# Latent attention with the values of two pairs of heads issued together, TensorE's order written by hand, and finished blocks parked in DRAM

## The chip, the cores and the metric

The kernel runs on one core of a Trainium2 chip. The metric is the device time of one execution in microseconds, lower is better; the median of several executions is compared between kernels.

## The reference

Two trunk layers of a diffusion backbone over 1024 latent tokens and 256 context tokens, width 1024, all in float32. Layer 0 mixes tokens by windowed grouped-query attention, layer 1 by gated linear attention, and each is followed by a squared-ReLU MLP. The change concerns layer 0's attention of the latent tokens alone:

```
def attend_block(args):                       # one block of 128 queries; 8 latent blocks
    q, k, v, blk = args                       # 16 query heads, 4 key/value heads of 64
    s_lat = einsum('bqhgd,bkhd->bhgqk', q, k)      # 3 * 128 keys: the block and its neighbours
    s_lat = where(in_window & in_sequence, s_lat, NEG_INF)
    s_ctx = einsum('bqhgd,bkhd->bhgqk', q, k_ctx)  # and all 256 context keys
    p = softmax_with_sink(concatenate([s_lat, s_ctx], -1), sink)
    return einsum(p_lat, v) + einsum(p_ctx, v_ctx)
y_lat = o_lat @ w_o
```

## The kernel before

Tokens are cut into ten blocks of 128: blocks 0 and 1 are context, 2 to 9 latent. First come the projections to queries, keys and values of all blocks, with the context blocks' own attention woven in (the listing's `ctx_rounds`), then the latent attention (`attention`), then the output projection with its residual and norm, block by block (`mixing`), then the MLP and layer 1.

`attention` is a generator that runs over 64 "pairs". A pair is one block `i`, one half `p` of the key/value heads and one `i4`; it holds two query heads (`e` = 0, 1) that use two key/value heads. One block has eight pairs. At step `t` it emits

- `scores` of pair t: for each of the two heads four matmuls (two parts of the query against the latent and the context keys) into a tile `sc` of two PSUM banks, of which there are two in all; VectorE then masks and takes the row's extreme (line 750), ScalarE takes the exponential (line 755), and GpSimd and ScalarE make the denominator;
- `divided` of pair t-1: VectorE's reciprocal (line 765), GpSimd's scaling of the probabilities (line 767);
- `turned` of pair t-3 (`LAG_T` = 3): ten transposes on TensorE (line 783; eight where the block has four key tiles), four, four and two of them into three banks `pt`, which VectorE (the first, line 786) and ScalarE (the others, line 788) empty into `pT`;
- `values` of pair t-4: ten (or eight) float32 matmuls on half of the array's columns each (the form 128*64 in the trace), two records each, into bank `o`, which gathers four pairs and is emptied by ScalarE into `oT[i]` (line 812);
- side work: once for four pairs the transposes of the next queries (bank `qt`, line 671, emptied by ScalarE at line 676 and twice by VectorE at line 680), once for eight those of further keys (`kt`), and on some steps a piece of the modulation sums (`mod_sums`, VectorE line 310) which at t = 30 and t = 62 ends in sixteen transposes `modT` (line 331).

The banks `pt`, `o`, `qt`, `kt` and `modT` come out of one pool of four (`ps1`). Working tiles of 4 KB for each partition come out of one pool of 45 (`u`); `oT[i]` holds one of them from the block's first half until its projection.

Who sets the order: the program is laid out by a planner that simulates it and gives each engine its ready instruction of highest rank, so instructions of one engine may stand in another order than they are emitted. Inside `manual_schedule(engines={PE})` TensorE's instructions keep the order in which they are emitted among themselves; instructions emitted outside may still be put between them, and the other engines stay with the planner. In the kernel before, the last three blocks' projections, with the first two steps of `attention`, lie in such a region; the remaining steps (`for _ in latents: pass`) do not.

Of the kernel before, what the change touches and what calls it, by code (L numbers as in the profile page):

```python
# [11 lines left out]
F32 = mybir.dt.float32  # L12
# [6 lines left out]
P = 128  # L19
# [6 lines left out]
NT = NC_T + NL_T  # L26
# [13 lines left out]
LAG_T = 3  # L40
# [124 lines left out]
class Backbone:  # L165
# [627 lines left out]
    def values(self, i, p, i4, pT):  # L793
        nc = self.nc
        ktiles = self.block(i)[4]
        if i4 == 0:
            self.po[i, p] = self.ps1("o")
        po = self.po[i, p]
        for n, tile_i in enumerate(ktiles):
            for e in range(2):  # L800
                g = 2 * p + e
                nc.tensor.matmul(  # L802
                    po[64 * e : 64 * (e + 1), P * i4 : P * (i4 + 1)],
                    self.kv[tile_i // 2][:, tile_i % 2, 256 + HD * g : 256 + HD * (g + 1)],
                    pT[e, n],
                    start=(n == 0),
                    stop=(n == len(ktiles) - 1),
                )
        if i4 == 3:
            if p == 0:  # L810
                self.oT[i] = self.u((P, 8, P), s="oT")
            nc.scalar.copy(self.oT[i][:, 4 * p : 4 * (p + 1), :], po.rearrange("p (a b) -> p a b", a=4))


    def scores_ctx(self, i, p, c, qs):
# [69 lines left out]

    def attention(self, steps, weights, o_ready):

        pairs = [(i, p, i4) for i in range(NC_T, NT) for p in range(2) for i4 in range(4)]
        qs, probs, pT = self.qs, {}, {}
        side = []  # L890
        for t in range(len(pairs) + LAG_T + 1):
            if t < len(pairs):
                i, p, i4 = pairs[t]
                probs[t] = self.scores(i, p, i4, qs[i, p])
            if 1 <= t <= len(pairs):
                self.divided(probs[t - 1])
            if 0 <= t - LAG_T < len(pairs):
                pT[t - LAG_T] = self.turned(pairs[t - LAG_T][0], probs.pop(t - LAG_T)["probs"])
            if 0 <= t - LAG_T - 1:
                self.values(*pairs[t - LAG_T - 1], pT.pop(t - LAG_T - 1))  # L900
            if t < len(pairs) and i4 == 0:

                nxt = (i, 1) if p == 0 else (i + 1, 0)
                q = self.queries(qs, *nxt) if nxt[0] < NT else []
                k = self.keys(i + 2) if p == 1 and i + 2 < NT else []
                side = [k[0:1], q[0:1] + k[1:2], q[1:2] + k[2:3], q[2:3] + k[3:4]]
                if p == 0 and i + 1 < NT:
                    self.q_back(i + 1)
            for f in side.pop(0) if side else ():
                f()  # L910
            if t in steps:
                steps[t]()
            if t >= len(pairs) - 20 and t % 4 == 0 or t >= len(pairs):
                weights.load()
            if t == len(pairs) - 1:
                o_ready()
            yield
# [539 lines left out]
    def gla_running(self, head, g, logs):  # L1457
# [5 lines left out]
        for d, lg in enumerate(logs):  # L1463
            run = self.half("run")[:, :w]
            r3 = run.rearrange("p (c t) -> p c t", t=P)
            l3 = lg.rearrange("p (c t) -> p c t", t=P)
            tot, mid = self.tot[head][:, d, self.chunks(g)], self.mid[head][:, d, self.chunks(g)]
            if d == 0:
                nc.vector.tensor_tensor_scan(run, self.reset[:, :w], lg, 0.0, ALU.mult, ALU.add)
                nc.vector.tensor_copy(mid, r3[:, :, 63])  # L1470
                nc.vector.tensor_copy(tot, r3[:, :, P - 1])
            else:
                nc.vector.memset(run[:, 0:1], 0.0)
                nc.vector.tensor_tensor_scan(
                    run[:, 1:w], lg[:, 0 : w - 1], self.reset[:, 1:w], 0.0, ALU.add, ALU.mult
                )
                nc.vector.tensor_copy(mid, r3[:, :, 64])
                nc.vector.tensor_tensor(tot, r3[:, :, P - 1], l3[:, :, P - 1], op=ALU.add)
            nc.vector.tensor_tensor(r3, r3, mid.unsqueeze(2).to_broadcast([P, nch, P]), op=ALU.subtract)
            if g > 0 or d == 0:  # L1480
                ex = self.u((P, 2, 512), s="ex")
            up, down = (ex[:, 0, :], ex[:, 1, :]) if g else (None, ex[:, d, :w])
            sgn = 1.0 if d == 0 else -1.0
            nc.scalar.activation(down, run, AF.Exp, scale=-sgn / TAU)
            if g > 0:
                nc.scalar.activation(up, run, AF.Exp, scale=sgn / TAU)
            res.append((up, down))
# [189 lines left out]
    def run(self):  # L1677
        nc, t = self.nc, self.t
        self.gm, self.pre = {}, {}
        self.q, self.oT = {}, {}  # L1680
        groups = [[0, 1], [2, 3, 4, 5], [6, 7, 8, 9]]


# [25 lines left out]
        def o_ready():  # L1709
            ready["rows"] = [self.gate_rows(0, 0, s) for s in range(2)]  # L1710
            ready["o"] = parts(0)
            ready["x"] = self.x_in(0)

        def parts(i):
            hi, lo = self.u((P, KT, P), F32R, "oh"), self.u((P, KT, P), F32R, "ol")
            self.split(self.oT[i], hi, lo)
            return hi, lo

        self.qs, self.qd = {}, {}
        latents = self.attention(steps, wo, o_ready)  # L1720
# [12 lines left out]
        with self.tc.manual_schedule(engines={mybir.EngineType.PE}):  # L1733
# [31 lines left out]
                    self.rotary(i)  # L1765
                    self.q_out(i)
            assert not ctx
        for _ in latents:
            pass
        rows = ready["rows"]  # L1770
        later = self.const([P, 768], "later", tag="rope")
        self.gnorm, self.junk = later[:, :DV], later[:, DV:].bitcast(mybir.dt.bfloat16)
# [1 line left out]
        h1 = MlpIn(self, 0, groups[1:], Acts(self, [[0, 1]]))  # L1774

        def mixing(tiles, parts, wo, x_of, row_of, keep, h, l, o, x, last):

            tiles = list(tiles)
# [18 lines left out]
            for s in range(n):  # L1797
                if s + 1 < n:
                    o[s + 1] = parts(tiles[s + 1])
                    x[s + 1] = x_of(tiles[s + 1])  # L1800

                def between():
                    if s >= 1:
                        residual(s - 1)
                    if s >= 2:
                        onward(s - 2)
                    if s >= 1:
                        normed(s - 1)

                y[s] = self.out_proj(o.pop(s), wo, between)  # L1810
                last(n - 1 - s)
# [4 lines left out]
        pairs = [(i, i + 4) for i in groups[1]]  # L1816
# [278 lines left out]
```

## Time and profile before

| what | us |
|---|---|
| median of three executions | 2607.4 (2607.23 to 2610.37) |
| the profiled execution, its own time | 2610.2 |
| its span | 2608.5 |
| the latent attention within the span | about 245 to 522 |

The span is the time from the first to the last instruction of the program. A stretch "284:317" is given in microseconds from the start of the span. PE stands for TensorE's matmuls, PEld for its weight loads, DVE for VectorE, ACT for ScalarE, POOL for GpSimd, SP for the queue that issues most transfers. Matmuls overlap in the records, so their spacing, from start to start, tells more than their durations.

### The profile page before, as it was taken

To read this page: it belongs to the slowest core of one execution; us is meant where nothing else is said; L and a number is where in the kernel's file an instruction comes from. 1 tells how busy PE (TensorE), PEld (TensorE's weight loads), DVE (VectorE), ACT (ScalarE), POOL (GpSimd) and SP (SyncE) were. 2 spreads that over 40 slices of the span, in tenths; PEclk is the share of its full clock that TensorE was granted. 3 is DMA by queue.
4 is the path that set the end of the run, shared out by engine and by line. 5 is a ranking of instruction groups with operands and counts; after the bars stand their busy time and mean duration, and the time that the engine had idled before them with its cause. 6 is when DMAs were issued, how large, how long until landed. Compare 5 with 4: busy or idle time off the path is not lost.

```text
span 2608.5 us, 36262 instructions
## 1 busy us (share of the span) xinstructions
PE 2543.1 (97%) x13523; PEld 2116.2 (81%) x13523; DVE 1714.7 (66%) x2607; ACT 1258.2 (48%) x2356; POOL 430.8 (17%) x720
## 2 busy tenths in 40 slices
PE   7999999999999999999999999999998999999998
PEld 5778888888888888788878888888887888878886
DVE  4775888757767665758868625636658656566676
ACT  3345777744644444433325535334446545445333
POOL 0354666411000000000002212212310000000002
PEclk9999999999999999999999999999999999999999
DMA  9210011222455565837245331102321554567474
GB/s 312 89 65 33 26 56 54 82 81 85 145 158 158 183 209 167 292 113 266 89 147 193 129 91 51 32 18 97 97 97 49 180 160 134 177 246 235 161 226 161
DMA packets 229856, 348.62 MB, mean 134 GB/s; under 512 B 24600, under 2 KB 123184, under 8 KB 229680
## 3 DMA queue, kind: packets, MB, share of 16 engines
q1 hardware_dynamic: 227088, 336.87, 39.8%
q0 software_dynamic: 2592, 9.44, 0.9%
q8 instruction: 106, 1.74, 0.3%
q14 instruction: 70, 0.57, 0.1%
HBM read 270.75 MB, written 75.50 MB: 133 GB/s over the span
## 4 chain that ended last, share of the span: by engine, by line
PE 85%; DVE 5%; DMA 4%; ACT 2%; issue 2%; POOL 1%; SPq 1%; DVEq 0%; POOLq 0%; ACTq 0%
PE p L229 7%; PE p L228 7%; PE p L230 6%; PE pa L229 4%; PE pa L228 4%; PE pa L230 4%; PE o L802 3%; PE y L230 3%; PE y L228 3%; PE y L229 3%; PE rp L228 2%; PE rp L229 2%; PE rp L230 2%; PE pc L228 2%; PE pc L230 2%; PE pt L783 2%
## 5 line engine op out<-in xcount | busy, mean ns | idle before, releaser
L229 PE MATMUL p<-ol,oh 128*128 128x512 f32 x896 | 350.7, 391 | 0.1
L230 PE MATMUL p<-oh,ol 128*128 128x512 f32 x896 | 347.2, 391 | 0.0
L228 PE MATMUL p<-oh 128*128 128x512 f32 x896 | 329.6, 392 | 4.9 <-ACT oh L212 4.1
L241 POOL TENSOR_SCALAR rs<-ss 128x1 f32<-128x1 f32 (+1 forms) x78 | 26.5, 340 | 1641.9 <-ACT later L235 1458.9
L213 DVE TENSOR_TENSOR ol<-wh,oh 128x1024 fp32r<-128x1024 f32 x128 | 153.5, 1222 | 94.3 <-ACT oh L212 93.9
L228 PEld LDWEIGHTS p<-oh 128*128 128x128 f32 x896 | 168.6, 189 | 44.1 <-ACT oh L212 5.4
L229 PEld LDWEIGHTS p<-ol,oh 128*128 128x128 f32 x896 | 168.9, 189 | 36.5 <-DVE ol L213 1.0
L230 PEld LDWEIGHTS p<-oh,ol 128*128 128x128 f32 x896 | 168.9, 189 | 35.3 <-issue 0.2
L212 ACT CAST oh<-wh 128x1024 fp32r<-128x1024 f32 x128 | 131.4, 1050 | 132.0 <-DVE wh L1212 27.6
L310 DVE SCALAR_TENSOR_TENSOR ma<-wm,cT,ma 128x1024 f32<-128x1024 f32 x112 | 147.2, 1345 | 47.0 <-DMA wm<-in_w_mod 47.0
L212 ACT CAST oh<-k 128x1024 fp32r<-128x1024 f32 x96 | 98.0, 1053 | 127.3 <-DMA k<-in_w_mlp_out 60.2
L213 DVE TENSOR_TENSOR wi<-wi,wi 128x512 fp32r<-128x512 f32 x176 | 116.6, 688 | 47.3 <-ACT wi L212 45.5
L1042 ACT COPY s<-pa 128x512 f32<-128x512 f32 x96 | 56.0, 585 | 185.5 <-PE pa L230 185.4
L767 POOL TENSOR_SCALAR pr<-pr,den 128x640 f32<-128x640 f32 (+2 forms) x160 | 124.3, 790 | 29.4 <-DVE den L765 16.6
L213 DVE TENSOR_TENSOR ol<-k,oh 128x1024 fp32r<-128x1024 f32 x96 | 113.9, 1224 | 21.2 <-ACT oh L212 17.3
L212 ACT CAST wi<-wi 128x512 fp32r<-128x512 f32 x176 | 103.4, 615 | 34.7 <-DMA hd<-h 20.9
L755 ACT ACTIVATE pr<-pr,nm 128x640 f32<-128x640 f32 (+1 forms) x128 | 102.5, 802 | 28.2 <-DVE nm L750 26.3
L228 PE MATMUL y<-woh,oh 128*128 128x512 f32 x288 | 113.9, 396 | 0.0
L230 PE MATMUL y<-woh,ol 128*128 128x512 f32 x288 | 112.4, 391 | 0.9 <-DVE ol L213 0.9
L229 PE MATMUL y<-wol,oh 128*128 128x512 f32 x288 | 112.2, 390 | 0.0
L229 PE MATMUL rp<-wgl,ah 128*128 128x512 f32 x288 | 112.1, 390 | 0.0
L230 PE MATMUL rp<-wgh,al 128*128 128x512 f32 x288 | 111.9, 390 | 0.0
(391 smaller groups left out, 6745.3 us busy)
## 6 DMA issues: line engine op xcount, KB each, us to landing
wm<-in_w_mod SPq DMA_DIRECT2D x96, 512.0 KB, 4.4
hd<-h SPq DMA_DIRECT2D x80, 512.0 KB, 3.0
wh<-hd SPq DMA_DIRECT2D x144, 256.0 KB, 3.7
wh<-in_w_mlp_out SPq DMA_DIRECT2D x144, 256.0 KB, 4.2
wi<-in_w_mlp_in SPq DMA_DIRECT2D x64, 512.0 KB, 5.0
k<-hd SPq DMA_DIRECT2D x80, 256.0 KB, 5.4
k<-in_w_mlp_out SPq DMA_DIRECT2D x80, 256.0 KB, 5.4
x<-in_x SPq DMA_DIRECT2D x16, 512.0 KB, 4.3
```

The lines of the kernel that those rows point to most:

```text
L212: self.nc.scalar.copy(hi, src)
L213: self.nc.vector.tensor_tensor(lo, src, hi.bitcast(F32), op=ALU.subtract)
L228: mm(out, a[0], b[0], start=start, stop=False, skip_group_check=onto)
L229: mm(out, a[0], b[1], start=False, stop=False, skip_group_check=onto)
L230: mm(out, a[1], b[0], start=False, stop=stop, skip_group_check=onto)
L241: nc.gpsimd.tensor_scalar(r, ss, inv_n, EPS, ALU.mult, ALU.add)
L310: nc.vector.scalar_tensor_tensor(acc[s], raw, c, acc[s], ALU.mult, ALU.add)
L755: nc.scalar.activation(pr, pr, AF.Exp, bias=nm[:, e : e + 1], scale=-1.0, accum_out=sums[:, e : e + 1])
L767: nc.gpsimd.tensor_scalar(pr, pr, den[:, e : e + 1], 0.0, ALU.mult, ALU.add)
L783: nc.tensor.transpose(pt[:, P * j : P * (j + 1)], probs[e][:, P * kt : P * (kt + 1)], self.ident)
L802: nc.tensor.matmul(po[64 * e : 64 * (e + 1), P * i4 : P * (i4 + 1)], self.kv[tile_i // 2][:, tile_i % 2, 256 + HD * g : 256 + HD * (g + 1) ...
L1042: nc.scalar.copy(s["s", j], s["pa"])
```

## The change

Three edits. `values` of pairs t-5 and t-4 are emitted together on every second step, in place of one on every step; the steps of the latent attention that were left to the planner are put into a region in which TensorE keeps the order of emission; and blocks 1 to 7 are written to DRAM (`od[i]`) when they are finished and read back into a fresh tile when `parts(i)` splits them for their projection. Blocks 0, 8 and 9 stay in SBUF. No arithmetic is added or removed.

```
@@ values
             nc.scalar.copy(self.oT[i][:, 4 * p : 4 * (p + 1), :], po.rearrange("p (a b) -> p a b", a=4))
+            if p == 1 and 0 < i < NT - 2:
+                self.od[i] = self.dp.tile([P, 8, P], F32, name=f"od{i}")
+                nc.sync.dma_start(self.od[i], self.oT.pop(i))
@@ attention
-            if 0 <= t - LAG_T - 1:
-                self.values(*pairs[t - LAG_T - 1], pT.pop(t - LAG_T - 1))
+            if t >= LAG_T + 2 and (t - LAG_T) % 2 == 0:
+
+                for n in (t - LAG_T - 2, t - LAG_T - 1):
+                    self.values(*pairs[n], pT.pop(n))
@@ run
-        self.q, self.oT = {}, {}
+        self.q, self.oT, self.od = {}, {}, {}
@@ run, parts
-            self.split(self.oT[i], hi, lo)
+            if i in self.od:
+                self.oT[i] = self.u((P, 8, P), s="oT")
+                nc.sync.dma_start(self.oT[i], self.od[i])
+            self.split(self.oT.pop(i), hi, lo)
@@ run
-        for _ in latents:
-            pass
+        with self.tc.manual_schedule(engines={mybir.EngineType.PE}):
+            for _ in latents:
+                pass
```

## Rows read from the trace of the kernel before

**Rows 1.** The page: busy time, share of the span and instructions of each engine, whole program.

```profile
PE 2543.1 (97%) x13523; PEld 2116.2 (81%) x13523; DVE 1714.7 (66%) x2607; ACT 1258.2 (48%) x2356; POOL 430.8 (17%) x720
```

**Rows 2.** Busy time of each engine by stretch. Each stretch is one latent block (eight pairs), from one emptying of bank `o` to another. Columns as the first line says.

```profile
core 0: us, PE busy (x) PEld busy (x) DVE busy (x) ACT busy (x) POOL busy (x), PEclk, DMA share, GB/s
284.00:317.00 33.00, 33.00 (x319) 28.96 (x319) 25.09 (x52) 24.83 (x67) 18.06 (x37) 1.00 0.12 36
317.00:352.00 35.00, 33.80 (x319) 28.89 (x318) 29.89 (x65) 27.04 (x72) 28.00 (x48) 1.00 0.16 50
352.00:390.00 38.00, 37.32 (x336) 31.22 (x335) 31.19 (x64) 25.04 (x65) 19.15 (x36) 1.00 0.15 43
390.00:423.00 33.00, 33.00 (x317) 28.63 (x316) 26.27 (x56) 25.45 (x68) 19.14 (x37) 1.00 0.17 49
423.00:455.00 32.00, 31.38 (x315) 27.73 (x314) 27.70 (x56) 26.36 (x68) 21.84 (x37) 1.00 0.25 67
455.00:488.00 33.00, 31.21 (x317) 27.24 (x317) 28.25 (x64) 26.95 (x68) 21.05 (x36) 1.00 0.17 47
```

**Rows 3.** TensorE's weight loads in order of time, around three turns from transposes to values and back. Columns: start, length of the run of equal instructions, engine, line, operation, tiles, shape, count, and in brackets the idle time before and what ended it.

```profile
352.69 1.12 PEld L783 LDWEIGHTS pt<-ident,pr 128*128 128x128 f32 x10
353.97 1.07 PEld L802 LDWEIGHTS o<-pT,kv 128*64 128x64 f32 x20 [0.16 <-issue]
355.21 0.30 PEld L736 LDWEIGHTS sc<-kl,qs 128*128 128x128 f32 x2 [0.17 <-issue]
...
356.39 0.90 PEld L783 LDWEIGHTS pt<-ident,pr 128*128 128x128 f32 x8
357.46 0.19 PEld L802 LDWEIGHTS o<-pT,kv 128*64 128x64 f32 x2 [0.17 <-issue]
```

**Rows 4.** The view of waits, stretch 245:522: who waited for whom, us in total, times, longest.

```profile
DVE den L765 <- POOL den L759: 16.3, 12, 1.9
...
PEld o L802 <- issue: 12.2, 72, 0.4
...
PEld pt L783 <- POOL pr L767: 5.2, 10, 1.2
...
PEld sc L736 <- DVE nm L750: 2.3, 9, 0.6
...
PEld sc L736 <- ACT pT L788: 1.7, 1, 1.7
```

**Rows 5.** Groups of instructions in the stretch 245:560: busy us, mean ns of one, and idle time of the engine before them.

```profile
L671 PE MATMUL qt<-ident,q 128*128 128x128 f32 x60 | 9.3, 278 | 0.0
...
L213 DVE TENSOR_TENSOR ol<-oT,oh 128x1024 fp32r<-128x1024 f32 x6 | 7.3, 1236 | 3.3 <-ACT oh L212 3.3
L212 ACT CAST oh<-oT 128x1024 fp32r<-128x1024 f32 x6 | 6.2, 1043 | 0.0
L331 PE MATMUL modT<-ident,ma 128*128 128x128 f32 x32 | 5.0, 279 | 0.0
```

**Rows 6.** TensorE's matmuls in order of time: the first visit to the values within the stretch (it is the context's), a turn of the next queries with what follows it, and the last visit. Columns as in rows 3.

```profile
244.78 1.09 PE L802 MATMUL o<-pT,kv 128*64 128x128 f32 x16
...
343.62 0.60 PE L671 MATMUL qt<-ident,q 128*128 128x128 f32 x4
344.06 0.60 PE L783 MATMUL pt<-ident,pr 128*128 128x128 f32 x4
...
344.95 0.66 PE L783 MATMUL pt<-ident,pr 128*128 128x128 f32 x4
345.54 1.31 PE L802 MATMUL o<-pT,kv 128*64 128x128 f32 x18
...
348.05 0.38 PE L783 MATMUL pt<-ident,pr 128*128 128x128 f32 x2
...
520.63 1.09 PE L802 MATMUL o<-pT,kv 128*64 128x128 f32 x16
```

**Rows 7.** ScalarE and VectorE at the same place, and after the transposes of rows 3: who empties the banks `qt` and `pt`, and when.

```profile
344.25 1.17 ACT L676 CAST qs<-qt 64x512 fp32r<-64x512 f32 x2 [1.24 <-PE qt L671]
...
345.75 0.69 DVE L786 COPY pT<-pt 128x512 f32<-128x512 f32 x1
...
346.46 1.39 DVE L680 TENSOR_TENSOR qs<-qt,qs 64x512 fp32r<-64x512 f32 x2
...
354.07 0.69 DVE L786 COPY pT<-pt 128x512 f32<-128x512 f32 x1
354.16 0.83 ACT L788 COPY pT<-pt 128x512 f32<-128x512 f32 x2
```

**Rows 8.** TensorE at the end of the sixteen transposes of a modulation vector.

```profile
370.56 0.60 PE L331 MATMUL modT<-ident,ma 128*128 128x128 f32 x4
371.84 1.25 PE L783 MATMUL pt<-ident,pr 128*128 128x128 f32 x8 [0.68 <-DVE S L332]
```

**Rows 9.** SP's queue, stretch 245:560: what its longest group of waits waited for (us in total, times, longest).

```profile
SPq L297 <- PE pt L783: 78.0, 7, 19.1
```

**Rows 10.** Transfers issued in 245:640: KB each, median us from issue to landing.

```profile
q<-qd SPq DMA_DIRECT2D x4, 512.0 KB, 3.3
```

**Rows 11.** The chain that ended last, at the start of two following blocks' norms in the output projection: start us, us, what.

```profile
539.86 0.87 PE xt L438 x8
...
551.64 0.87 PE xt L438 x8
```

## The prediction

> **What bounds the kernel now.** I read the page's engine line first: TensorE is busy for 97% of the span, the next engine for 66% [rows 1]. Then the table by stretch, to see whether that holds where the change is. In the six latent blocks from 284 to 488 us the granted clock is full, TensorE has hardly an idle microsecond, VectorE is busy for 168.4 of the 204 us and ScalarE for 155.7 [rows 2]. So TensorE sets the pace there too; one block of eight pairs takes 34 us, four pairs 17.0.
>
> The weight loads say what TensorE does with that time. Transposes follow each other every 0.109 us (eight of them and the turn after them take 1.07), one pair's scores take 1.18 (355.21 to 356.39), one pair's values 1.09. But at every turn from full-width work to the half-column values, and at every turn back, the row shows 0.16 or 0.17 us of idle time with no engine named [rows 3]; over the stretch the entries alone are 12.2 us in 72 rows, 0.17 each [rows 4]. A visit to the values therefore costs about 0.35 us beyond its work. I counted the visits along the listing of TensorE from 244.78 to 520.63: 91, of which one is the context's, so 90 for 64 pairs [rows 6]. The planner splits many visits, because it slips values into gaps.
>
> The account closes: for four pairs 4 x (1.18 + 1.09 + 1.09) = 13.4, the next queries' four transposes 0.44 [rows 6], every second time as much for keys, 0.22 on average, and 90/16 = 5.6 visits at 0.35, 2.0. That is 16.1 of 17.0. Real waits make up most of the rest: those on GpSimd's probabilities, VectorE's minima and ScalarE's copies are the largest, 9.2 us in the stretch [rows 4].
>
> **What the change removes.** 64 pairs in twos are 32 visits, and a fixed order forbids splits: 90 - 32 = 58 visits fewer, 58 x 0.35 = 20.3 us off TensorE's own path. The lower bound is the idle time alone, 58 x 0.33 = 19.1; the upper one takes a full 0.20 for each turn (1.28 us for ten transposes and the turn, less 1.09 [rows 3]), 23.2. I take 20.3. Of the 9.2 us of waits the fixed order may keep all or, if its own pauses give the other engines time to catch up, none; I take half, a gain of 4.6.
>
> **What the fixed order adds.** The planner used its freedom at one place that matters: the four small banks. After the queries' transposes the trace shows four transposes of a pair, four more, and the last two only at 348.05, after eighteen records of values and a pair's scores [rows 6]. They waited for a bank: bank `qt` was full from 343.62 until VectorE's second reading of it ended at 347.85 [rows 7], bank `o` was held, and two remained for three. TensorE lost little, since other work went ahead. In the new order nothing may. On step 4m+1 it does scores, transposes, a double visit and the queries' transposes; on step 4m+2 scores, then ten transposes with `qt` and `o` still held (`o` is opened by the first double visit and closed by the one on step 4m+3). The third bank has to wait until the first or second is emptied.
>
> Its price: in a run of ten from 352.69 the eighth transpose is issued by 353.56; the first bank was emptied at 354.76 by VectorE, the second near 354.73 by ScalarE [rows 3, 7]. So 1.17 us. The low end is a copy that starts at once: the fourth transpose is through at 353.13, 0.69 more is 353.82, 0.26 late. The high end is the release of `qt`: 4.23 us after it began, while the third bank is due 0.44 + 1.18 + 0.87 = 2.49 after, 1.74. There are 15 such steps (60 transposes, four each [rows 5]): 3.9 to 26.1. I take 1.0 each, 15.0, near the first figure, with a little off because a pause of TensorE is just what lets VectorE come forward.
>
> The sixteen transposes of a modulation vector stand in a row too, with two banks free, and each bank waits for VectorE; today one of the two vectors shows a wait of 0.68 [rows 8]. Between nothing and 2 x 4 x 0.68 = 5.4 I take 2.0.
>
> **What it moves.** Values come one step later for every even pair; nothing waits for them but `oT`, and the last double visit is on the same step as the last single one now. Their `pT` tiles live a step longer, one working tile more. At the end of the attention the first projection's matmuls are emitted outside the region, so the planner can go on putting them between, and the drain of the last three pairs stays covered; without that cover it would cost one emptying, about 1.2 us.
>
> **The parking** adds seven stores and seven loads of 512 KB on SP's queue, each some 3.3 us to landing by the nearest row [rows 10], with the DMA engines at 0.12 to 0.25 of their time [rows 2]. Behind a store that waits for the copy into `oT` stand the modulation weights, the next block's queries and the output weights; SP's queue already stands up to 19.1 us at a time for a free tile [rows 9] without stopping TensorE, so I cost it at nothing. A load is issued a whole projection ahead; blocks follow each other every 11.78 us [rows 11] and load and split take 3.3 + 1.04 + 1.24 = 5.6 [rows 5, 10]. Uncovered it would be 5.6 once, for block 1. The tiles that come free shorten SP's waits, which is worth nothing while TensorE has work.
>
> **The sum.** -20.3 - 4.6 + 15.0 + 2.0 = -7.9 us. The profiled execution took 2610.2, its span 2608.5; it is the slowest of the three shown, whose median is 2607.4. The difference applied to the median gives 2599.5; to the profiled time, 2602.3. What can be told from no change in this kernel is about 0.2%, 5.2 us, so the forecast lies just outside.
>
> **The rule that weighs against it.** The six blocks keep VectorE busy for 168.4 us; its waits on the denominator, 16.3 in the stretch [rows 4] or 12 in the six blocks, don't shrink with TensorE. 180 of 204 is then the least those blocks can take, 24 us less than now, and with some of them the floor is near whatever TensorE saves. The Trainium skill, "TensorEngine Tiling (Array Packing)", section "PSUM Bottleneck", says that tiling quickens TensorE but not the emptying of PSUM, so that the copies may become the limit. By that rule alone the kernel would take 2583; the trace bears it out so far as VectorE's and ScalarE's shares go.
>
> **Rivals.**
> *The emptying engines set the pace, and the banks cost little.* If the planner puts the copies of `pt` first, the wait is 0.26 x 15 = 3.9 and the modulation costs nothing: -20.3 - 4.6 + 3.9 = -21, near VectorE's floor of -24. Time 2583 to 2590. For it: VectorE's idle 35.6 us in the six blocks. Against: in the rows its copy stands behind two readings of scores. Chance 0.18.
> *The bank gives back what the visits save.* At 1.17 to 1.74 for each of the 15 steps, and the old waits all kept, -20.3 + 17.6 + 2 = -0.7 up to +7.8. Time about 2605. Chance 0.21.
> *Slower.* The same wait comes on both short stretches of a group: `qt` is read a second time only on step 4m+3's side work, and if VectorE, fuller than now, takes scores first, the transposes of 4m+3 find two banks too. 30 x 1.17 = 35.1: -20.3 - 4.6 + 35.1 + 2 = +12, 2620. It decides from 23 us on, that is 0.76 us for each of 30. Chance 0.20.
>
> **How the numbers follow.** The forecast has 0.41, with 2592 to 2602 as its own range; the likeliest single time in it is 2599. Faster by over 0.2%: forecast and first rival, 0.59, less 0.01 for its edge, 0.58. Within 0.2%: 0.22. Slower: 0.20. The range goes from 2581 (a little below the first rival) to 2617 (into the slower one), which leaves some 0.2 out.
>
> **What would show it.** Visits to line 802's group down from 90 to 32, the entries named "issue" from 72 to about 32; the last copy into `oT` some 8 us earlier than now; VectorE's share in the middle blocks up from 0.83 towards 0.87. New waits of TensorE before transposes, ended by the copies of `pT` or the second reading of `qt`, about 1 us long and some 15 of them: if they are absent the time is 2585, if there are 30 it is over 2607. Blocks of the projection still every 11.8 us. The prediction is wrong if probabilities come late instead (waits on line 767), or if the planner, given another order, lays out a later stage differently: nothing in this trace prices that.

## The result: slower by 0.4%

| | before | after |
|---|---|---|
| median, us (both measured on one chip) | 2608.3 | 2616.7 |
| ratio, 95% interval | | 1.0036 (1.0025 to 1.0046) |
| span of the profiled execution, us | 2608.5 | 2614.6 |
| its own time, us | 2610.2 | 2616.6 |

The forecast was 2599, faster. The range of 2581 to 2617 just holds the time; the sign is wrong.

The page of the kernel after, its engine line, against [rows 1]: TensorE's instructions are the same in number, 11 us less busy in the matmul records, in a span 6 us longer.

```profile
PE 2532.2 (97%) x13523; PEld 2118.8 (81%) x13523; DVE 1714.9 (66%) x2607; ACT 1256.4 (48%) x2356; POOL 427.2 (16%) x720
```

After, busy time by stretch, the same six stretches as [rows 2] and their sum in one window; columns as there.

```profile
284.00:317.00 33.00, 30.87 (x325) 28.80 (x323) 26.87 (x59) 25.76 (x68) 19.05 (x40) 1.00 0.21 65
317.00:352.00 35.00, 30.91 (x313) 29.01 (x312) 29.31 (x60) 25.80 (x67) 27.43 (x47) 0.95 0.20 66
352.00:390.00 38.00, 33.46 (x342) 30.54 (x341) 31.26 (x66) 25.95 (x68) 18.89 (x38) 1.00 0.18 56
390.00:423.00 33.00, 30.87 (x323) 28.81 (x322) 27.02 (x59) 26.15 (x70) 19.33 (x40) 1.00 0.16 52
423.00:455.00 32.00, 27.32 (x257) 24.72 (x258) 24.63 (x48) 23.39 (x60) 18.12 (x31) 0.95 0.28 81
455.00:488.00 33.00, 28.73 (x292) 26.34 (x292) 25.46 (x54) 24.20 (x60) 18.15 (x31) 0.95 0.29 80
284.00:488.00 204.00, 182.16 (x1839) 168.22 (x1836) 164.55 (x341) 151.25 (x389) 120.97 (x222) 0.97 0.22 66
```

TensorE, which was idle for some 4 of these 204 us before, is now idle for 22 of them; VectorE and ScalarE, which the change was to drive harder, do less work than before in the same time. In three stretches the granted clock is below 1.00, where it was full throughout. TensorE is busy least in the two last, 27.3 of 32 and 28.7 of 33 us, where the output weights are loaded beside the stores and the DMA share is highest (0.28 and 0.29).

After, the view of waits over the latent attention (240:529), against [rows 4].

```profile
...
DVE den L765 <- POOL den L759: 30.5, 19, 2.0
...
PEld sc L736 <- DVE nm L750: 10.6, 15, 2.6
DVE wol L213 <- ACT woh L212: 10.3, 5, 3.4
...
PEld pt L783 <- ACT pT L788: 8.9, 6, 2.2
...
PEld pt L783 <- DVE qs L680: 6.7, 4, 3.1
...
PEld o L802 <- issue: 5.4, 28, 0.4
```

The entries into the values (the last line) fell in number from 72 to 28, as they should. Above them stand three waits of TensorE that were small or absent: at the scores for VectorE's minima, 10.6 us where it was 2.3, and at the transposes for a bank that ScalarE or VectorE has yet to empty, 15.6 us where the kernel before has none of any size.

For all kernels below I made one account from TensorE's weight loads. The stage runs from the first scores to the last copy into `oT`. A visit is an entry into the values. A wait is a gap between two loads beyond their usual spacing that ends with an event on another engine or a transfer (the releaser); "half clock" is what loads lose by following each other at twice their spacing. All but the counts in us. The waits are counted a little differently from the view of waits, and a single profiled execution stands behind each line. Three of the kernels, e13 to e15, leave a part of the arithmetic out; the runs are explained below.

| kernel | stage | visits | waits | at the scores | half clock | after the stage |
|---|---|---|---|---|---|---|
| before | 279.7 | 91 | 12.0 | 2.4 | 0.5 | 2086.7 |
| after | 288.6 | 35 | 36.4 | 11.4 | 4.8 | 2086.3 |
| order alone (e1) | 285.4 | 65 | 28.0 | 3.3 | 1.5 | 2079.9 |
| values in twos and parking, planner's order (e2) | 280.2 | 68 | 18.6 | 11.2 | 2.8 | 2084.4 |
| after, third bank late (e3) | 286.4 | 35 | 38.4 | 18.0 | 1.9 | 2085.9 |
| after, no parking (e10) | 283.4 | 35 | 34.5 | 6.6 | 2.9 | 2085.7 |
| third bank late, no parking (e12) | 283.1 | 35 | 35.0 | 16.4 | 2.3 | 2083.5 |
| order alone, third bank late (e9) | 282.4 | 65 | 26.0 | 8.7 | 0.5 | 2089.4 |
| before, no reciprocal (e13) | 275.2 | 90 | 8.0 | 3.4 | 0.5 | 2084.4 |
| e2, no reciprocal (e14) | 273.1 | 62 | 17.2 | 9.6 | 0.7 | 2081.7 |
| e12, no reciprocal (e15) | 281.0 | 35 | 34.3 | 15.7 | 0.7 | 2085.2 |
| e12, heads apart (e17) | 283.0 | 35 | 37.7 | 12.6 | 0.6 | 2084.7 |

Before to after: 56 visits fewer at 0.35 are -19.6, waits +24.4, half clock +4.3: +9.1, and the stage is 8.9 longer. It began 2.4 us earlier, so the span grew by 6.1. The price of 0.35 is the one read before the change; that the sum closes supports it. The last column shows how far single executions can be trusted: hardly any run edits what lies there, and it goes from 2079.9 to 2089.4. A difference of a few us between two stages of this table settles nothing by itself.

### The profile page after: what moved, and what is told of

Read it like the earlier page. It is cut to its first block, busy times and chain, and to the rows that moved or that the text cites. A ratio compares the mean times of both kernels' runs of the same rounds, so it can differ in the third digit from the quotient of the medians.

```text
span 2614.6 us, 36293 instructions
## 1 busy us (share of the span) xinstructions
PE 2532.2 (97%) x13523; PEld 2118.8 (81%) x13523; DVE 1714.9 (66%) x2607; ACT 1256.4 (48%) x2356; POOL 427.2 (16%) x720
## 3 DMA queue, kind: packets, MB, share of 16 engines
q8 instruction: 106, 1.74, 0.3%
## 4 chain that ended last, share of the span: by engine, by line
PE 84%; DVE 7%; DMA 4%; issue 2%; ACT 2%; POOL 1%; SPq 0%; DVEq 0%; POOLq 0%; ACTq 0%
PE p L228 7%; PE p L229 7%; PE p L230 7%; PE pa L229 4%; PE pa L228 4%; PE pa L230 4%; PE y L230 3%; PE y L229 2%; PE y L228 2%; PE rp L230 2%; PE rp L229 2%; PE rp L228 2%; PE o L802 2%; PE pc L228 2%; PE pc L230 2%; PE pc L229 2%
```

## The experiments

### Which of the three edits costs the time

The fixed order alone, in the kernel before, and the other two edits alone, in the planner's order:

```
  e1: before, with      with manual_schedule(engines={PE}): for _ in latents: pass
  e2: after, without it (for _ in latents: pass)
  e8: as e2, and values of one pair on every step again (parking alone)
```

> The kernel before with one edit: TensorE's fixed order for the remaining steps of the latent attention; values one pair at a time, nothing parked. Theory A (the fixed order makes the pair's last two transposes wait for the third bank after each turn of the queries, about 1.2 to 1.5 us on 11 to 15 steps, and adds waits of the scores for VectorE): visits fall from 90 to 64, 26 x 0.35 = 9 us, waits grow by 20 to 30; 2617 to 2630. Theory B (the pairing is to blame: a short step followed by a long one leaves VectorE behind): without pairing the fixed order is harmless, 2596 to 2606.

> The changed kernel without its fixed order: values of two pairs are emitted together, blocks are parked, and the planner orders TensorE. Theory A: the planner goes round the bank as before, so the waits stay near 12 us; visits fall to 35 to 60 because it may still split them, 11 to 19 us saved; 2590 to 2599. Theory B: the pairing itself starves VectorE or the tiles, 2606 to 2618.

> The kernel before with blocks 1 to 7 parked in DRAM and nothing else. By the forecast's step: nothing, 2603 to 2612. Rival: SP's queue, in order, puts the parked blocks between loads that TensorE needs, or the tiles set free let the planner run further ahead; then more than 5 us either way, with the difference inside the attention or the projection after it.

Measured: e1 2609.3, ratio 1.0014 (1.0004 to 1.0023); e2 2607.3, 1.0000 (0.9991 to 1.0009); e8 2609.2, 1.0005 (0.9996 to 1.0015). Neither half makes the 0.36% by itself. Order alone, the view of waits of its latent attention (239:525):

```profile
PEld pt L783 <- ACT pT L788: 9.8, 6, 2.1
...
PEld pt L783 <- DVE qs L680: 6.2, 5, 1.7
...
PEld sc L736 <- DVE nm L750: 3.2, 7, 1.0
```

and values in twos with parking in the planner's order, the same view:

```profile
PEld sc L736 <- DVE nm L750: 10.7, 18, 1.8
```

So the bank wait belongs to the fixed order (16 us with single values too), and the wait at the scores comes with the values in twos (10.7 us in the planner's order too). e2 also parks, and no run has the values in twos alone in the planner's order; with parking alone (e8) the same line shows 3.6 us. The planner, given values in twos, still splits them: 68 visits. It wins 8 us by the visits and pays 6.6 in waits and 2.3 at half clock. e1's stage is 5.7 us longer, its time only by 0.14%. The 6.8 us by which its profiled execution is shorter after the stage are no gain of the order. TensorE's matmuls follow each other there as before but for a few, and about 4 us arise at four places (from 942, 1424, 1970 and 2308 us in the kernel before) where the execution before ran at a granted clock of 0.50 and that of e1 at 1.00. e1's profiled execution is the fastest of its eleven (2606.35), and that of the kernel before lies above its median. Parking in the planner's order costs nothing that can be told (up to 0.15% by its interval).

### The bank wait: is it the cause?

At the place that the prediction worked out. After, TensorE's weight loads around one step 4m+2 (columns as in rows 3):

```profile
343.08 0.90 PEld L783 LDWEIGHTS pt<-ident,pr 128*128 128x128 f32 x8
345.41 0.20 PEld L783 LDWEIGHTS pt<-ident,pr 128*128 128x128 f32 x2 [1.44 <-ACT pT L788]
345.58 0.30 PEld L736 LDWEIGHTS sc<-kl,qs 128*128 128x128 f32 x2
```

and VectorE over it:

```profile
342.90 0.89 DVE L750 CUSTOM_DVE_ANT_0 pr<-sc,mask,nsink 128x640 f32<-128x640 f32 x1 [0.82 <-PE sc L739]
...
343.71 0.88 DVE L750 CUSTOM_DVE_ANT_0 pr<-sc,mask,nsink 128x640 f32<-128x640 f32 x1
...
344.63 1.39 DVE L680 TENSOR_TENSOR qs<-qt,qs 64x512 fp32r<-64x512 f32 x2
346.06 0.69 DVE L786 COPY pT<-pt 128x512 f32<-128x512 f32 x1
```

Eight transposes, a stop of 1.44 us, two transposes. VectorE comes to its bank only at 346.06, after two minima and the readings of `qt`; ScalarE's copy of the other (344.77, behind an exponential) lets TensorE go on. To take the wait away without touching the arithmetic, e3 writes the two last transposes of a pair behind the values, or ahead of the next pair's:

```
+  def one(c, part): ...                      # bank, transposes, copy, as before
+  for c, part in enumerate(parts[:2]): one(c, part)
+  self.third = [lambda ...: one(c + 2, part) for c, part in enumerate(parts[2:])]
   # attention: the list is run ahead of `turned` on a step with values, and behind the values
```

> The changed kernel with the order written so that a pair's last two transposes (the third bank) come later: those of an odd pair after the next step's scores, those of an even pair after the double visit. Nothing else. Theory A: the 15 or so waits before the third bank, some 20 us with the half-clock stretch that the longest brings, go away; 2594 to 2601, and the view of waits no longer shows transposes ended by the copies of pT or the reading of qt. Rival C (VectorE and ScalarE are the limit, the bank is only where TensorE notices): the same time is waited elsewhere, before the scores; 2611 to 2617.

> The kernel before with TensorE's order fixed, values one pair at a time, no parking, and the third bank's transposes of a pair written after the next step's scores. Theory F (the fixed order costs the bank, the pairing costs VectorE: a short step gives it too little time between two pairs' scores): without pairing the late third bank has its full effect, TensorE's waits fall from 28 us (order alone) to 8 to 15, visits 64; the attention ends 8 to 14 us earlier than in the run with the order alone, 2593 to 2602. Rival C (the engines that empty are the limit, wherever TensorE waits): as with pairing, the waits come back before the scores; 2606 to 2614.

e9 is the same with single values and no parking. Measured: e3 2614.3, 1.0030 (1.0019 to 1.0042); e9 2609.4, 1.0009 (1.0000 to 1.0017). The waits of e3 (240:527; its lines 784 and 789 are 783 and 788 of the change):

```profile
PEld sc L736 <- DVE nm L750: 16.2, 25, 2.5
...
PE pt L784 <- ACT pT L789: 2.9, 4, 0.8
PEld pt L784 <- POOL den L759: 2.9, 6, 0.9
```

Most of the bank wait is gone (2.9 us of TensorE's matmuls for ScalarE's copy are left, in four waits), and nothing was won that can be told from the change: TensorE now waits longer at the scores, and for GpSimd at the transposes, 38.4 us in all where it was 36.4. The bank wait was real, but taking it away let TensorE meet the other engines at the next place.

### VectorE's extra work and its reciprocal

The pieces of the modulation sums are extra work of VectorE on steps without values in the change; e4 moves them to steps with values. e5 to e7 take the latent attention's reciprocal off VectorE, where it waits 30 us for GpSimd's denominator in the change, and give it to GpSimd, in the change, in e3, and in the kernel before. (The lines that keep the context's reciprocal where it was are not shown.)

```
  e4:  - range(14, 64, 4)                    + range(15, 64, 4)
  e5, e6, e7:  - nc.vector.reciprocal(den, den)
               + nc.gpsimd.tensor_tensor(den, den, self.mone, op=ALU.pow)     # mone: -1
```

> The changed kernel with the pieces of the modulation sums moved from steps 14, 18, ... 62 to steps 15, 19, ... 63, that is from short steps to steps with a double visit. Theory A: the bank's 20 us stay, the scores' waits for VectorE (12 us) fall by a third to a half; 2610 to 2614. Rival C (VectorE is the limit): spreading its work takes most of the waits away, the bank's too; 2598 to 2606.

> The changed kernel with the latent attention's reciprocal of the denominator taken off VectorE: GpSimd raises it to the power -1 (as it does for the norms, 0.62 us for one column) before it scales the probabilities. Theory D (VectorE, in order, stands 29 us before this reciprocal, twice what it did, and so reads scores and empties banks late): the scores' waits for VectorE fall from 11 us to under 4, the bank's stay but shorten; 2603 to 2611. Rival E (GpSimd becomes the late one, its 40 us more come into the chain of every pair): TensorE waits 15 us or more for probabilities; 2615 to 2630.

> The changed kernel with both edits: the third bank's transposes late, as in the run named late third, and the reciprocal on GpSimd. Theory D: with the bank out of the way and VectorE free of the denominator most of TensorE's 38 us of waits go; 2588 to 2600, faster than the kernel before. Rival E: the probabilities come late; 2612 to 2625. If the bank and VectorE were only two names for one limit: 2605 to 2612.

> The kernel before with the reciprocal on GpSimd alone, as the control. Theory D: there the planner works round VectorE's waits and TensorE waits little, so the time moves by less than 5 us, 2602 to 2611. Rival E: 2612 or more.

Measured: e4 2622.4, 1.0056 (1.0042 to 1.0070); e5 2621.9, 1.0052 (1.0037 to 1.0067); e6 2619.9, 1.0044 (1.0028 to 1.0061); e7 2607.7, 1.0001 (0.9991 to 1.0010). e4 is worse than the change: waits at the scores 17.2 us, where they were 11.4. e5 and e6 are no better than what they came from, though VectorE lost 10 us of work and those waits; GpSimd was busy 46 us longer in 240:530 in e5 than in the change. As GpSimd took more time, this didn't yet say whether VectorE's wait matters.

e13 to e15 leave the reciprocal out altogether, in the kernel before, in e2 and in e12 (the probabilities are multiplied by the denominator); e16 keeps it and divides a pair one step later.

```
  e13, e14, e15:  - nc.vector.reciprocal(den, den)          # of the latent attention
  e16 (from e12): - self.divided(probs[t - 1])   + self.divided(probs[t - 2])
```

> The kernel before with the latent attention's reciprocal (line 765) left out, so that the probabilities are multiplied by the denominator itself: VectorE loses 64 x 0.16 = 10 us of work and, above all, never stands waiting for GpSimd's denominator (16.3 us in 12 waits before). It is the control for the next two. Theory 1 (what refuses the gain is VectorE standing in order behind a denominator, with the next scores' minimum behind it): little here, since TensorE waits only 2.4 us for VectorE; 2605 to 2607. Rival 2 (the wait is set elsewhere, by the chain of copies and readings itself): the same, 2607.

> Values in twos and the parking in the planner's order (as in the run of these alone, which came out equal to before), with the reciprocal left out. Theory 1: TensorE's waits at the scores for VectorE fall from 11.2 us to under 4, and the visits' gain appears: 6 to 9 us under the control, about 2599. Rival 2: the waits stay near 10 us and the time within 2 us of the control.

> Values in twos in the fixed order, third-bank transposes written later, no parking, with the reciprocal left out (with it: 2609.7, 16.4 us of waits at the scores for VectorE). Theory 1: those waits fall below 6 us and the time is 8 to 12 us under the control, about 2597. Rival 2: the waits stay above 12 us, 2607 to 2609.

> As the kernel before it with the reciprocal kept, but the division of a pair emitted one step later (at step t for pair t-2 in place of t-1), so that the denominator has a whole step more to arrive; a complete computation. Theory 1: VectorE's waits for the denominator (26.7 us there) mostly go, and the time comes near that of the run without the reciprocal, plus its 10 us of VectorE work: about 2602. Against it: the scaled probabilities have one step less to reach their transposes, so TensorE may wait for GpSimd (line 767) instead; then 2610 or more. Rival 2: no change, 2609.

Measured: e13 2602.8, 0.9983 (0.9973 to 0.9992); e14 2600.4, 0.9972 (0.9961 to 0.9982); e15 2609.0, 1.0004 (0.9995 to 1.0013); e16 2611.7, 1.0016 (1.0007 to 1.0026). The wait at the scores in e14, then in e15:

```profile
PEld sc L736 <- DVE nm L750: 8.0, 18, 1.4
```

```profile
PEld sc L736 <- DVE nm L750: 13.2, 23, 1.6
```

The theory falls in the form in which I put it. Without the reciprocal the waits at the scores stay, and the control gained 5 us by itself. Of e14's 7 us only the difference to the control, 2.3 us between the medians, can be the values in twos (with the parking); taken directly, the eight executions against the ten, it is 1 to 6 us, under the 6 to 9 that the theory asked for. What the runs do show is that the reciprocal is worth 5 us in the kernel before and 7 with values in twos in the planner's order, and in the fixed order no more than some 2 (e15 against e12, with overlapping intervals). Leaving it out also frees GpSimd from waiting for it, so they don't tell whether VectorE's work, its wait or GpSimd's is worth the time.

### Uneven steps

Sorted by the step on which they fall, 9.5 of the 16.4 us at the scores in e12 are 24 waits of 0.4 us on average at the second head, right after a step with transposes and no values. There TensorE has some 2.1 us of work, and VectorE 2.5 for the pair (two minima at 0.81, a copy of 0.69, a reciprocal of 0.16); the two tiles of scores both belong to one pair. e17 (from e12) and e18 (from the change without parking) issue the second head's scores behind the eight or ten transposes on the steps that have values:

```
+  probs[t] = self.scores(i, p, i4, qs[i, p], apart)       # apart: first head's scores only
   ... divided, turned ...
+  if apart: probs[t]["second"]()                          # the second head's
```

> The fixed order with values in twos, third-bank transposes late and no parking (2609.7 before this edit), in which on the steps that have values the second head's scores are issued after the pair's eight transposes instead of before them. Theory 3 (uneven steps): on a step without values TensorE has 1.18 us of scores and 0.87 to 1.09 of transposes, less than VectorE's two minima, copy and reciprocal of 2 x 0.81 + 0.69 + 0.16 = 2.5 us, and since the two tiles of scores both belong to the pair before, the next step's second head waits 0.4 us; 24 such waits, 9.5 of the 16.4 us at the scores. Then those waits go, the stage is about 9 us shorter, and the time is 2600 to 2602. Theory 4 (VectorE and the exponentials are simply full, whatever the order): the waits move to the transposes (for probabilities or for banks) and the time stays at 2608 to 2611.

> The same edit in the change as it is, without the parking (2611.0 before this edit): the third-bank transposes stay where the change has them. Here only 3.5 of 6.6 us of waits at the scores are of this kind, because the bank wait (19.5 us) already gives VectorE its time. Theory 3: 3 us less at the scores, the bank wait unchanged, 2607 to 2609. Theory 4: 2611.

Measured: e17 2612.6, 1.0016 (1.0007 to 1.0025); e18 2613.9, 1.0027 (1.0018 to 1.0036). The waits at the scores fell in e17 from 16.4 to 12.6 us, not by 9.5, and some 6 us came at the transposes, for banks that ScalarE and VectorE empty and for GpSimd's keys; all waits together went from 35.0 to 37.7. In e18 they rose. Unevenness of this kind doesn't explain the waits.

The 0.4 us are a mean of unlike waits. Of e12's waits at the second head four, of 1.5 to 2.5 us, make up about 7 us (they end at 267.31, 298.08, 332.50 and 402.24), and nearly all others are 0.2 or less. Before each of the four, the minimum that is waited for stands behind VectorE's two readings of `qt` (line 680, 1.39 us; from 265.08, 295.71, 330.13 and 399.87). The same readings stand before the bank stop at 345.41 shown above. In the change they lie within or at most 1.5 us ahead of 12 of TensorE's 20 weight-load waits over 0.7 us, 19.5 of 30.3 us. No run moved them, so whether they are the cause was not tested.

### The parking

> The changed kernel without the parking (finished blocks stay in SBUF). Theory G (the stores stand at the head of SP's queue, up to 28.9 us, and hold up the loads of weights behind them, whose splitting in order holds VectorE): the scores' waits for VectorE fall from 11 us to 5 or less, 2606 to 2611. Rival H (the pairing needs the tiles that the parking sets free): waits grow towards the end of the attention, 2619 to 2630. Neither: 2613 to 2619.

> The changed kernel with the seven stores issued from ScalarE's queue, right behind the copy that they store, in place of SP's. Theory G: SP's queue no longer stands before them and the loads come in time, 2607 to 2612. Otherwise 2613 to 2619.

> The run named late third without the parking: order and pairing stay. Theory G: 2598 to 2608, since both the bank and the stores are out of the way. Theory F (the pairing itself): the scores still wait 12 us or more for VectorE, 2611 to 2618. Rival H: over 2618.

```
  e10 (from after), e12 (from e3): the store of od[i] left out, so the load is too
  e11 (from after):  - nc.sync.dma_start(self.od[i], ...)  + nc.scalar.dma_start(self.od[i], ...)
```

Measured: e10 2611.0, 1.0015 (1.0006 to 1.0024); e11 2611.0, 1.0011 (1.0001 to 1.0020); e12 2609.7, 1.0013 (1.0004 to 1.0023). Three comparisons agree: leaving the parking out saves 5.7 us of the change and 4.6 of e3, and leaving it in but issuing its store from ScalarE's queue saves 5.7 too. So it is not the transfer that costs, but where its issue stands. SP's queue after, its waits in 243:560, then its issues in order of time:

```profile
SPq L815 <- ACT oT L812: 79.5, 4, 28.9
SPq L815 <- ACT den L758: 61.2, 3, 21.0
```

```profile
438.51 0.33 SPq L297 DMA_DIRECT2D wm<-in_w_mod  x1
458.57 0.33 SPq L815 DMA_DIRECT2D od<-oT  x1
459.00 1.19 SPq L220 DMA_DIRECT2D wor<-in_attn_w_o  x2
```

The same queue without parking (e10):

```profile
443.04 0.33 SPq L297 DMA_DIRECT2D wm<-in_w_mod  x1
452.18 1.45 SPq L220 DMA_DIRECT2D wor<-in_attn_w_o  x2
```

The store stands at the head of the queue until ScalarE has copied the block (457.98), 20 us after the issue before it. The output weights go out right behind it, 6.8 us later than without it, and in company with it. What that did, all engines after:

```profile
464.16 1.05 ACT L212 CAST woh<-wor 128x1024 fp32r<-128x1024 f32 x1 [1.67 <-DMA wor<-in_attn_w_o]
...
464.35 0.66 PE L671 MATMUL qt<-ident,q 128*128 128x128 f32 x4
...
465.23 1.23 DVE L213 TENSOR_TENSOR wol<-wor,woh 128x1024 fp32r<-128x1024 f32 x1 [2.66 <-ACT woh L212]
...
466.38 0.88 DVE L750 CUSTOM_DVE_ANT_0 pr<-sc,mask,nsink 128x640 f32<-128x640 f32 x1
...
467.32 0.62 PE L736 MATMUL sc<-kl,qs 128*128 128x384 f32 x2 [2.31 <-DVE nm L750]
```

The weights land at about 464.16, 5.2 us after their issue. ScalarE's cast waits for them, VectorE's split waits for the cast, the scores' minima stand behind the split, and TensorE, which in its fixed order has nothing else to do, stops for 2.31 us. Such casts wait 4.2 us for transfers in the change (243:530) and not at all in e10. In the planner's order (e8) the same store costs nothing that the times can tell (0.9996 to 1.0015), though the stage of its one profiled execution is some 4 us longer than before.

## Why the prediction was wrong

**Right, with their sizes.** The visits: 58 fewer forecast, 56 found, 19.6 us of 20.3 at the same price. The third bank: 15.0 us forecast, 15.6 found in the view of waits, for ScalarE's copy and `qt` as named. The wait is right, the closeness of the sum is luck: there are 10 of 1.56 us where I had 15 of 1.0. The modulation's transposes: 2.0 forecast, 2.6 found.

**The step that failed first**: "Of the 9.2 us of waits the fixed order may keep all or, if its own pauses give the other engines time to catch up, none; I take half, a gain of 4.6." I bounded the old waits by nothing and by themselves; that they could grow was left out of both ends, without a reason. All waits that are neither bank nor modulation went from about 11 to about 18 us, +7 where I had -4.6; those at the scores alone grew by 9. That is 12 us; the forecast (-7.9) and the difference of the medians (+8.4) lie 16 apart, and the next step, 4, is the rest but for terms under 1 and the stage's earlier start.

**The step that was missing**: TensorE's clock. The change loses 4.8 us at half clock, the kernel before 0.5 (last section). No term of the sum had it. It isn't an accident of the profiled execution: the mean granted clock is 0.991 to 0.993 in all six executions of the change, and 0.993 to 0.996 in 21 of the kernel before that ran beside e1.

**The step that was costed at nothing**: the parking. I argued that SP's queue stands up to 19.1 us without stopping TensorE [rows 9]. With the planner's order behind the queue no cost can be told (e8); in the fixed order it is 4.6 to 5.7 us (e10 to e12). These are no further term but lie within the two above: with the parking TensorE waits 4.8 us longer at the scores and 2.9 less elsewhere (36.4 us in all against 34.5), and loses 1.9 us more at half clock (4.8 against 2.9).

**The rule.** The Trainium skill, "TensorEngine Tiling (Array Packing)", section "PSUM Bottleneck", warns that the copies may become the limit when tiling quickens TensorE. The runs agree with its direction, though TensorE was relieved here by fewer turns and not by smaller tiles: 19.6 us of visits went, and its waits, mostly for engines that empty PSUM, rose from 12.0 to 36.4 us. The floor that I drew from VectorE's busy share (180 of 204 us) was not reached, and its premise failed: VectorE's waits for the denominator, counted as fixed, rose from 16.3 to 30.5 us. No engine is full in the table by stretch, yet no arrangement with the whole arithmetic went under the kernel before.

**The rivals.** "The bank gives back what the visits save" had the price of one wait right (1.17 to 1.74; 1.56 found), not the number of waits. Its sum of -0.7 to +7.8 gives 2606.7 to 2615.2 and not the "about 2605" beside it. "Slower" had the sign and named VectorE, but asked for 30 waits at the transposes; 10 came there, and the rest of the loss at the scores and from the clock. The upper end of the range was drawn into that rival, so that it just holds 2616.7 is luck too. In e3 and e12, taking the waits at the banks away brought waits elsewhere in nearly the same amount.

**What stays open.** Visits at 0.35, waits and half clock together are 44 us in the kernel before and 45 in e2, and 49 to 54 in every fixed order with the whole arithmetic (e1, e3, e9, e10, e12, e17, after), whatever is moved. This points to something other than TensorE's own work that sets the length of this stage, which was argued from these sums and not shown by taking it away. The path through the reciprocal is part of it in the planner's order (e13, e14), but hardly in the fixed one (e15). Which loop through VectorE, ScalarE and GpSimd it is was not settled; VectorE's readings of `qt` are the nearest rival that no run tests. No complete kernel tried is faster than the one before.

## What to carry to other kernels

An engine that is 97% busy is not alone in setting the pace when the next ones wait for it only now and then: before crediting time taken off it, ask what it will run into, and let the waits that are there now grow as well as shrink. In a hand-fixed order a late arrival can become a stop, so a transfer that waits for a result shouldn't stand ahead of loads on the same queue; issuing it from the queue of the engine that makes the result took the whole cost away here. If taking one wait away only makes another appear, compare the sum of waits, not their names; and look at the single waits before explaining their mean.

## What the runs showed that was not expected

After its three longest stops TensorE ran at the lower of its two clocks. After, by stretch (columns as in rows 2): two of the stops, each with what followed it, and the time around the end of the third.

```profile
325.00:327.70 2.70, 0.00 (x0) 0.00 (x0) 2.65 (x6) 1.47 (x4) 2.70 (x3) 1.00 0.39 72
328.30:331.50 3.20, 3.20 (x15) 3.20 (x14) 2.79 (x6) 2.21 (x5) 3.20 (x6) 0.50 0.69 277
...
464.90:467.30 2.40, 0.10 (x1) 0.00 (x0) 2.07 (x4) 1.84 (x4) 0.00 (x0) 1.00 0.60 167
467.90:471.20 3.30, 3.30 (x16) 3.14 (x15) 3.22 (x8) 1.29 (x5) 0.39 (x2) 0.53 0.03 5
...
263.60:266.60 3.00, 2.83 (x12) 2.53 (x12) 3.00 (x9) 0.82 (x2) 3.00 (x6) 0.50 0.00 0
```

The granted clock is 0.50 of full, 1.2 GHz, in the second row and the last, and 0.53 in the fourth, whose ends are a little wide. It fell at no fixed distance from the end of the stop: before TensorE took up work again at 263.76 (last row), shortly after 327.87, and 0.8 us after 467.32. Ten transposes took 2.32 us behind the stop at 467.32 instead of 1.25 (346.87), 1.1 us more. There are four such places in this kernel's latent attention, 4.8 us in all. Three are at the stops of 2.30, 2.90 and 2.31 us, the fourth, from 430.7 on, is at two of 1.68 and 0.86 us with little work between. After the following stops, among others, the clock stayed at 1.00 (TensorE's matmuls in order of time):

```profile
415.00 0.44 PE L783 MATMUL pt<-ident,pr 128*128 128x128 f32 x2 [1.20 <-ACT pT L788]
...
452.28 0.44 PE L783 MATMUL pt<-ident,pr 128*128 128x128 f32 x2 [2.01 <-ACT pT L788]
```

The length of a stop alone doesn't settle it, though: in e1 the clock fell at one of 1.88 us, in e2 at one of 1.56, and in e10 not at one of 2.11. So two orders with nearly the same sum of waits can differ by what the clock adds: e3 waits 38.4 us and loses 1.9 at half clock, the change 36.4 and 4.8. That many short waits are cheaper than a few long ones is not shown.
